# Down projection: fourteen of 22 pairs per half by seven products, their sums stored through GpSimd's queue, and weights laid out as tiles on the host

## The chip, the cores and the metric

The kernel runs on one core of one Trainium2 chip. The time is device time in microseconds (us). A core has TensorE (PE, matrix products into PSUM), VectorE (DVE), ScalarE (ACT), GpSimd (POOL) and SyncE (SP). DMAs are issued from the queues of SP, ACT and POOL and are carried out by 16 DMA engines. An engine executes its instructions in the order in which they were issued to it; a DMA queue issues its DMAs in order, and a DMA that waits holds up those behind it.

## The reference, cut to what matters

One layer of an encoder with batch 1, 256 tokens and 2048 features. Its last third is a gated channel mixer with a centred convolution of 3 taps over the tokens, a residual and a gate:

```python
def conv_glu(hn, w_up, conv_w, conv_b, w_down):      # hn (256, 2048), w_up (2048, 2*5632), w_down (5632, 2048)
    up = hn @ w_up
    gate, val = jnp.split(up, 2, axis=-1)
    gate = dwconv_centred(gate, conv_w, conv_b)      # 3 taps along the tokens, per feature
    return (jax.nn.gelu(gate, approximate=True) * val) @ w_down

# in the layer, after the mixer
hn = rmsnorm(h, ffn_norm_pre)
h = h + rmsnorm(conv_glu(hn, ...), ffn_norm_post)
gate = jax.nn.sigmoid(rmsnorm(h, ple_norm_pre) @ w_ple_gate)
h = h + rmsnorm(gate * (p @ w_ple), ple_norm_post)
```

`rmsnorm(x, g)` is x times 1/sqrt(mean of x squared over the features + 1e-6) times g. In front of this stands a mixer of a bidirectional state-space scan and a pooling part, with an input projection (`w_in`) and an output projection (`w_out`). All inputs are float32.

## The kernel before

**Products.** Each float32 operand is split into a high part, which TensorE's fp32r format holds, and the rest; a product of two operands is three products on PE (high x high, high x low, low x high). `split` (line 141) does this for a weight piece of up to 1024 columns: ACT copies the high part, DVE subtracts. The results lie in two pools of five buffers each, `whi` and `wlo`, that all weight pieces take in turn. The raw weights come through three buffers `raw` of 8 KB per partition.

**Stages.** In order: the input projection in three parts (`dtu`, `xbc`, `z`, 0 to 199 us of the span), the output projection `wo`, the embedding's first half `ple`, the up projection (293 to 789 us, eleven slabs of 512 gate features and 512 value features; `ga`, `va`), the down projection (`dn`, 789 to 1017 us, two halves of 1024 output columns), the embedding's second half, and the gate (`gt`, two halves).

**Up.** Each slab has two half slabs of gate and two of value features, computed features by tokens. `feature_pairs` (line 340) multiplies a half slab's weights, four splits, with the normalised input; after each two splits `aside` takes one list from `work` (line 194) and issues its jobs. `total` adds the two PSUM parts. The gate is multiplied by `rfb`, the row factor of the norm along the tokens; `conv` (line 416) applies the three taps, the middle one with the bias on ACT, the others as DVE scalar-tensor-tensor operations (line 428); ACT computes gelu; DVE multiplies the result by `rfb` (line 885), which belongs to the value half, and then by the value. The result stays in pages `hid` (features by tokens, six pages of 8 KB per partition).

**Down.** `token_major` (line 291) goes through 22 pairs of 128-row weight blocks for each half; its operand of 128 features by 128 tokens is the stationary one, 512 weight columns move. A regular pair takes 2 blocks x 2 token halves x 2 column halves x 3 = 24 products. For the pairs in `fast`, `seven_products` (line 239) treats the pair as a 2 x 2 block product and forms it with seven block products instead of eight (Strassen's scheme in Winograd's form), so 21 products; `combine` (line 269) then puts the accumulators right once for all of a half's such pairs. It needs four sums of activation blocks (`pair_sums`, line 774: four DVE operations on 128 columns, a split of 512 columns) and four sums of weight blocks (`add_blocks`, line 232).

The sums of weight blocks don't depend on the activations. For the down and gate pairs they are made during the up stage, as jobs in `work`: `block_sums` (line 208) has a `fetch`, two steps later an `add`, and one step later a `store` to DRAM, all DMAs on SP's queue; the last two stay in their pages. In the down stage a pair by seven products then loads its sums (a page of 1 MB, `t`) and the two blocks of raw weights that are used unsummed (1536 columns, two DMAs). The activation sums are made in `hid_sums` (line 920) when the pair comes, by DVE and ACT; those of the four pairs in `dn_keep` stay in two pages for the second half.

**Buffers.** There are 13 pages of 8 KB per partition for everything large, three buffers `mid` of 4 KB, two `hs` of 4 KB in the late part, and one `junk` of 2 KB.

**Order.** The source issues in program order, and a planner that works with expected times orders each engine's and each queue's instructions from it; `issue_after` and `load` (line 116) tie DMAs to the weight loads, except those marked as free to go ahead. `at` gives actions that are issued ahead of a pair: in the down stage's second half `back` at pair 13 (the residual `h` returns from DRAM, two DMAs of 1 MB) and `first_gate` at pair 16 (the first pair of gate weights: loaded once through SP, and once more by a POOL DMA that adds it to a negated copy, so that the low part is made without DVE; lines 943 to 952).

**DRAM layout.** The weights lie in DRAM as given. A tile of 128 partitions is gathered from rows of the matrix: pieces of 1 KB for the up weights, 2 KB for `xbc` and 4 KB for most others.

Of the kernel before, what the change touches and what calls it, by code (L numbers as in the profile page):

```python
# [11 lines left out]
F32 = mybir.dt.float32  # L12
# [39 lines left out]
def build(nc, a, out):  # L52
    x = a["x"][0]
    w_in, w_out, w_up = a["w_in"][0], a["w_out"][0], a["w_ffn_up"][0]
    w_down, w_gate, w_ple = a["w_ffn_down"][0], a["w_ple_gate"][0], a["w_ple"][0]
    out = out[0]

    with tile.TileContext(nc) as tc, \
# [37 lines left out]
        c_dt = DSSD + 1536  # L96
        r0 = wp.tile([P, 2048], F32, tag="raw", bufs=3, name="dtur0")
        for n in range(2):
            first = ins(nc.scalar.dma_start(r0[:, n * 352:(n + 1) * 352],
                                            w_in[:P, c_dt + n * 352:c_dt + (n + 1) * 352]))  # L100
# [55 lines left out]
        def raw(name, src, a_, b_):  # L156
            r = wp.tile([P, 2048], F32, tag="raw", bufs=3, name=name)
            if src is None:
                return r
            last["dma"] = load(r[:, :a_ * b_].rearrange("p (a b) -> p a b", a=a_), src, True)  # L160
            return r
# [46 lines left out]
        def block_sums(name, w, c0, k, held):  # L208


            pg = []

            def fetch():
                r = page(f"{name}b{c0}_{k}")
                pg.append(r)
                load(r.rearrange("p (k c) -> p k c", k=2),
                     w[k * P:(k + 2) * P, c0:c0 + 1024].rearrange("(k p) c -> p k c", p=P))

            def add():
                add_blocks(pg[0])  # L220
                if held:
                    sums_[name, c0, k] = pg[0], True

            def store():
                if not held:
                    t = dp.tile([P, 2048], F32, tag=f"{name}s{c0}_{k}", bufs=1, name=f"{name}s{c0}_{k}")
                    load(t, pg[0])
                    sums_[name, c0, k] = t, False

            return [fetch], [], [add], [store]  # L230

        def add_blocks(r):

            v = r.rearrange("p (b c) -> p b c", b=4)
            nc.vector.tensor_add(v[:, 0:2], v[:, 0:2], v[:, 1::2])  # L235
            nc.vector.tensor_add(v[:, 3], v[:, 3], v[:, 0])
            nc.vector.tensor_add(v[:, 2], v[:, 2], v[:, 3])

        def seven_products(name, stage, w, k0, c0, a_, acc, alt, start, stop):
# [3 lines left out]
            if (stage, c0, k0) in sums_:  # L243
                r = raw(f"{name}r", None, 0, 0)
                last["dma"] = load(r[:, 512:1536], w[(k0 + 1) * P:(k0 + 2) * P, c0:c0 + 1024], True)
                last["dma"] = load(r[:, :512], w[k0 * P:(k0 + 1) * P, c0:c0 + 512], True)
# [4 lines left out]
                b11 = split(f"{name}a", r[:, :512], 512)  # L251
                b2 = split(f"{name}b", r[:, 512:1536], 1024)
            else:
                r = t = raw(f"{name}r", w[k0 * P:(k0 + 2) * P, c0:c0 + 1024]
                            .rearrange("(k p) c -> p k c", p=P), 2, 1024)
                b11 = split(f"{name}a", r[:, :512], 512)
                b2 = split(f"{name}b", r[:, 1024:], 1024)
                add_blocks(r)
            t13 = split(f"{name}c", t[:, :1024], 1024)
            t42 = split(f"{name}d", t[:, 1024:], 1024)  # L260
            for x, (wh, wl), c, o, own in (
                    ("a11", b11, 0, alt[0], True), ("a12", b2, 0, acc[0][0], False), ("s4", b2, 512, acc[0][1], False),
                    ("s1", t13, 0, alt[1], True), ("s3", t13, 512, alt[2], True), ("a22", t42, 0, acc[1][0], False),
                    ("s2", t42, 512, alt[3], True)):
# [26 lines left out]
        def token_major(name, w, c0, ks, get, acc, tail=1, fast=(), alt=None, sums=None, at=()):  # L291
# [3 lines left out]
            for u in range(nu):  # L295
# [3 lines left out]
                if u in fast:  # L299
                    if u == fast[0]:  # L300
# [3 lines left out]
                r = None if f"{name}{k0}_0" in ready else raw(f"{name}r{k0}", w[k0 * P:(k0 + 2) * P, c0:c0 + 1024]  # L304
                                                               .rearrange("(k p) c -> p k c", p=P), 2, 1024)
# [8 lines left out]
                for t, (o, c), (k, wh, wl), q in order:  # L314
                    xh, xl = (v[:, t * P:(t + 1) * P] for v in get(k))
                    xx, ww = ((xh, wh), (xh, wl), (xl, wh))[q]
                    mm(o, xx, ww[:, c:c + o.shape[-1]], k == ks[0] and q == 0, k == ks[-1] and q == 2)
# [3 lines left out]
                aside()  # L321

        def feature_major(name, w, c0, get, acc):

            for u in range(4):
                r = raw(f"{name}r{u}", w[u * 512:(u + 1) * 512, c0:c0 + 512]
                        .rearrange("(k p) c -> p k c", p=P), 4, 512)
# [12 lines left out]
        def feature_pairs(name, w, c0, get, acc):  # L340


            for u in range(2):
                r = raw(f"{name}r{u}", w[u * 1024:(u + 1) * 1024, c0:c0 + 256]
                        .rearrange("(k p) c -> p k c", p=P), 8, 256)
# [97 lines left out]
        for u in range(0, NK, 2):  # L443
            r = [wp.tile([P, 2048], F32, tag="raw", bufs=3, name=f"dtur{u}") if u else r0, page(f"dtur{u + 1}")]
            for j in range(2):
                k = u + j
                if k == 0:
                    last["dma"] = load(r[0][:, 704:1056], w_in[:P, c_dt + 704:c_dt + 1056])
# [3 lines left out]
                for c0, c1 in ((0, 704), (704, 1056)) if k == 1 else ((0, 1056),):  # L452
                    last["dma"] = load(r[j][:, c0:c1], w_in[k * P:(k + 1) * P, c_dt + c0:c_dt + c1])
# [29 lines left out]
        with tc.issue_after(half[0]), tc.issue_after(half[1]):  # L483
# [11 lines left out]
            for a_ in range(4):  # L495
# [17 lines left out]
        load(pmat.rearrange("p (g s t) -> p g s t", g=4, s=2),  # L513
             a["pool_matrix"].rearrange("g (s p) t -> p g s t", p=P))
        poolw = page("poolw")
        load(poolw.rearrange("p (g c d) -> p g c d", g=4, c=2),
             a["pool_w"][0].rearrange("g (c p) d -> p g c d", p=P))
# [122 lines left out]
        def xbc(slab):  # L640
            acc = main(f"xbc{slab}")
            feature_major(f"xb{slab}", w_in, DSSD + slab * 512, hn, acc)
# [88 lines left out]
        token_major("z", w_in, 0, list(range(NK)), hn, zacc)  # L731
# [42 lines left out]
        def pair_sums(name, s, o, a11, a21, a12, a22):  # L774

            s1, s2, s3, s4 = (s[:, i * P:(i + 1) * P] for i in range(4))
# [5 lines left out]
            nc.vector.tensor_sub(o[:, 512:], s[:, :512], o[:, :512].bitcast(F32))  # L782
            return {f"s{i + 1}": (o[:, i * P:(i + 1) * P], o[:, 512 + i * P:512 + (i + 1) * P]) for i in range(4)}
# [22 lines left out]
        def sublayer(name, w, ks, get, gain, h, vnext, panel=Panel, fast=((), ()), sums=None, at=()):  # L806
# [3 lines left out]
            for half in range(2):  # L810
# [6 lines left out]
                for t in range(2):  # L817
                    for n in range(2):
# [4 lines left out]
                        nc.scalar.activation(junk, b, AF.Square, accum_out=q)  # L823
                        nc.vector.tensor_mul(mg[t][:, c], b, gain[:, c])
# [40 lines left out]
        dn_fast, gt_fast, dn_keep = ((2, 3, 5, 7, 8, 10, 12, 13, 15, 16, 18, 19), (2, 3, 5, 7, 8, 10, 12, 13, 15, 16, 18, 19)), ((4, 6), (1, 2)), (3, 8, 13, 18)  # L865
# [4 lines left out]
        for i, w_ in enumerate(which[2:] + which[:2]):  # L870
            for j, jobs in enumerate(block_sums(*w_, i >= len(which) - 2)):
                work[3 * i + 2 + j].extend(jobs)
        hid = []
        for s in range(DFF // 512):
            sc = mid(f"gr{s}")
            for i in range(2):
                ga = main(f"ga{s}{i}")
                feature_pairs(f"ug{s}{i}", w_up, s * 512 + i * 256, hf, ga)
# [4 lines left out]
            cv = conv(f"fc{s}", sc, 3, V_FCW + 4 * s, NF, V_FCB + 4 * s)  # L883
            nc.scalar.activation(cv, cv, AF.Gelu_apprx_tanh)
            nc.vector.tensor_tensor(cv.rearrange("p (f t) -> p f t", f=4), cv.rearrange("p (f t) -> p f t", f=4),
                                    rfb.unsqueeze(1).to_broadcast([P, 4, L]), op=ALU.mult)
            for i in range(2):
                va = main(f"va{s}{i}")
                feature_pairs(f"uv{s}{i}", w_up, DFF + s * 512 + i * 256, hf, va)
# [9 lines left out]
        def get_hid(k):  # L899
            if k % 2 == 0:  # L900
                t = lp.tile([P, 1024], F32R, tag="hs", bufs=2, name=f"hs{k}")
                src = hid[k // 8][:, (k % 8) * L:(k % 8 + 2) * L]
# [187 lines left out]
```

## Time and profile before

| | us |
|---|---|
| median of 3 runs | 1122.9 (1122.65 to 1123.32) |
| the profiled execution | 1123.46 |
| its span, first to last instruction | 1121.6 |

Busy time by stage in that execution, in us of the stretch:

| stretch | stage | PE | DVE | ACT | DMA share | GB/s |
|---|---|---|---|---|---|---|
| 0 to 50 | dtu | 48.5 | 26.7 | 37.6 | 0.99 | 369 |
| 50 to 143 | xbc | 92.2 | 76.1 | 61.4 | 0.45 | 152 |
| 143 to 199 | z | 56.0 | 46.9 | 28.5 | 0.59 | 207 |
| 199 to 293 | wo, ple | 94.0 | 83.3 | 52.5 | 0.60 | 190 |
| 293 to 789 | up | 495.5 | 400.7 | 257.4 | 0.93 | 307 |
| 789 to 903 | down, first half | 114.0 | 105.6 | 82.2 | 0.76 | 259 |
| 903 to 1017 | down, second half | 114.0 | 105.0 | 84.4 | 0.92 | 325 |
| 1017 to 1121 | ple, gate, end | 97.1 | 83.8 | 61.4 | | |

Matmul ends are modelled, so PE's busy share does not say that it runs at its full pace; the pace is read from the chain of waits, which gives the start of each string of products and their number. Line 87 is the helper that records every product, line 152 and 153 the two halves of `split`, line 119 every load; groups with these lines are told apart by the names of their tiles (`dn04ah`: half 0 of the down stage, block 4, first split, high part). The clock granted to PE was 0.999 on the mean.

### The profile page before, as it was taken

The numbers are of one execution on the slowest core, as the hardware profiler recorded it, in microseconds if no ns is written. First come the engines' busy times: TensorE is split into PE (matmuls) and PEld (weight loads), VectorE is DVE, ScalarE is ACT, GpSimd is POOL, SyncE is SP. The second block draws the span as 40 slices with busy tenths as digits, with TensorE's granted clock in tenths as the row PEclk, the third lists the DMA queues.
The fourth block names the chain that finished last, engine by engine and source line by source line (L and its number), as shares of the span: only waits on it lengthen the run. The fifth ranks groups of instructions, "written<-read, shape, count | busy, mean of one in ns | idle before, by whom it ended". The sixth has DMA issues, their size and how long they took to land.

```text
span 1121.6 us, 15747 instructions
## 1 busy us (share of the span) xinstructions
PE 1111.2 (99%) x5975; PEld 957.1 (85%) x5975; DVE 928.0 (83%) x1291; ACT 665.4 (59%) x929; POOL 31.1 (3%) x69
## 2 busy tenths in 40 slices
PE   9999999999999999999999999999999999999997
PEld 9999988888888888888888888888888888888876
DVE  6468897799898877877877768878799999899795
ACT  6848663555764554554545545545677777786673
POOL 0200000100100000000000000000000000001001
PEclk9999999999999999999999999999999999999999
DMA  9853447456799989999999898996969688995673
GB/s 361 312 197 104 162 161 277 151 188 189 252 320 349 316 298 340 303 295 313 341 319 310 289 335 303 313 297 218 321 198 336 219 292 295 381 323 175 231 235 107
DMA packets 145996, 300.87 MB, mean 268 GB/s; under 512 B 5504, under 2 KB 98560, under 8 KB 137856
## 3 DMA queue, kind: packets, MB, share of 16 engines
q1 hardware_dynamic: 145216, 298.19, 78.8%
q0 software_dynamic: 272, 1.05, 0.5%
q8 instruction: 47, 0.77, 0.3%
q10 hardware_dynamic: 432, 0.62, 0.2%
q14 instruction: 29, 0.24, 0.1%
HBM read 268.38 MB, written 31.46 MB: 267 GB/s over the span
## 4 chain that ended last, share of the span: by engine, by line
PE 95%; ACT 2%; DVE 1%; issue 1%; DMA 0%; POOL 0%; SPq 0%; POOLq 0%; ACTq 0%
PE va L87 22%; PE ga L87 21%; PE dna L87 14%; PE woa L87 7%; PE xbc L87 6%; PE gt L87 5%; PE z L87 4%; PE dtu L87 4%; PE dns L87 3%; PE dn0s L87 1%; PE dn1s L87 1%; PE ple L87 1%; PE pw L87 1%; PE yd L87 1%; DMA dtur<-w_in 0%
## 5 line engine op out<-in xcount | busy, mean ns | idle before, releaser
L87 PE MATMUL ga<-wox,ug_0h 128*128 128x512 f32 x352 | 125.5, 395 | 0.0
L87 PE MATMUL ga<-wox,ug_1h 128*128 128x512 f32 x352 | 125.1, 394 | 0.0
L87 PE MATMUL va<-wox,uv_1h 128*128 128x512 f32 x352 | 124.8, 393 | 0.0
L87 PE MATMUL va<-wox,uv_0h 128*128 128x512 f32 x352 | 124.8, 393 | 0.0
L87 PE MATMUL ga<-wox,ug_1l 128*128 128x256 f32 x352 | 99.2, 282 | 0.0
L87 PE MATMUL ga<-wox,ug_0l 128*128 128x256 f32 x352 | 99.1, 282 | 0.0
L87 PE MATMUL va<-wox,uv_1l 128*128 128x256 f32 x352 | 99.1, 281 | 0.0
L87 PE MATMUL va<-wox,uv_0l 128*128 128x256 f32 x352 | 99.1, 281 | 0.0
L87 PEld LDWEIGHTS va<-wox,uv_1h 128*128 128x128 f32 x352 | 66.1, 188 | 15.0
L87 PEld LDWEIGHTS va<-wox,uv_0h 128*128 128x128 f32 x352 | 66.1, 188 | 15.0
L87 PEld LDWEIGHTS ga<-wox,ug_0h 128*128 128x128 f32 x352 | 66.1, 188 | 14.9
L87 PEld LDWEIGHTS ga<-wox,ug_1h 128*128 128x128 f32 x352 | 66.1, 188 | 14.9
L87 PEld LDWEIGHTS ga<-wox,ug_0l 128*128 128x128 f32 x352 | 66.2, 188 | 0.1
L87 PEld LDWEIGHTS ga<-wox,ug_1l 128*128 128x128 f32 x352 | 66.2, 188 | 0.0
L87 PEld LDWEIGHTS va<-wox,uv_1l 128*128 128x128 f32 x352 | 66.2, 188 | 0.0
L87 PEld LDWEIGHTS va<-wox,uv_0l 128*128 128x128 f32 x352 | 66.2, 188 | 0.0
L87 PE MATMUL dna<-dn_0h,hs 128*128 128x512 f32 x160 | 50.1, 393 | 0.0
L87 PE MATMUL dna<-dn_1h,hs 128*128 128x512 f32 x160 | 49.9, 393 | 0.0
L235 DVE TENSOR_TENSOR dnb<-dnb 128x1024 f32<-128x1024 f32 x24 | 29.3, 1222 | 14.0 <-DMA dnb<-w_ffn_down 14.0
L903 ACT CAST hs<-hid 128x512 fp32r<-128x512 f32 x44 | 27.1, 617 | 18.3 <-PE dna L87 18.3
L904 DVE TENSOR_TENSOR hs<-hid,hs 128x512 fp32r<-128x512 f32 x44 | 30.2, 686 | 9.1 <-ACT hs L903 9.0
L428 DVE SCALAR_TENSOR_TENSOR fc<-gr,vt,fc 128x255 f32<-128x255 f32 x88 | 36.8, 479 | 0.1
(1909 smaller groups left out, 3060.3 us busy)
## 6 DMA issues: line engine op xcount, KB each, us to landing
dnb<-w_ffn_down SPq DMA_DIRECT2D x24, 1024.0 KB, 10.3
dns<-dnb SPq DMA_DIRECT2D x22, 1024.0 KB, 6.9
dn0r<-w_ffn_down SPq DMA_DIRECT2D x10, 1024.0 KB, 6.2
dn1r<-w_ffn_down SPq DMA_DIRECT2D x10, 1024.0 KB, 6.9
zr<-w_in SPq DMA_DIRECT2D x8, 1024.0 KB, 5.2
dtur<-w_in SPq DMA_DIRECT2D x14, 528.0 KB, 8.5
wo0r<-w_out SPq DMA_DIRECT2D x7, 1024.0 KB, 5.5
wo1r<-w_out SPq DMA_DIRECT2D x6, 1024.0 KB, 5.7
```

What stands on the lines that cost most here:

```text
L87: last["pe"] = ins(nc.tensor.matmul(o, lhsT, rhs, start=start, stop=stop, skip_group_check=True))
L235: nc.vector.tensor_add(v[:, 0:2], v[:, 0:2], v[:, 1::2])
L428: nc.vector.scalar_tensor_tensor(o[:, lo:hi], i[:, lo + d:hi + d], vec(wcol + j * wstep + f), o[:, lo:hi], op0=ALU.mult, op1=ALU.add)
L903: nc.scalar.copy(t[:, :512], src)
L904: nc.vector.tensor_sub(t[:, 512:], src, t[:, :512].bitcast(F32))
```

## The change

Six edits:

1. `dn_fast` has 14 pairs per half instead of 12, so runs of 4, 3, 3, 2 and 2 pairs. The products of a pair come in another order: the sums that were third and fourth in the split order change places, and the four products of `acc` are spread differently. `add_blocks` is four additions of 512 columns.
2. `block_sums` stores through POOL's queue. 30 of 32 sums are stored; the jobs lie 11/4 steps apart instead of 3. In the down stage a pair's raw weights are one DMA instead of two.
3. The activation sums of eight pairs (`dn_stored`) are made in the up stage, in an `hs` buffer, and stored by a POOL DMA of 0.5 MB; each half loads them again with a POOL DMA into a `mid` buffer. The other six pairs make theirs in each half, with `junk` as scratch. The two pages of `dn_keep` go.
4. The multiplication by `rfb` after gelu goes. The row factor comes in at the evacuation of the down projection, where a row is a token (`row=rf`).
5. The taps of the up stage are ACT operations with a scale into `cv`, `tp` and, in place, `sc`, and two DVE additions over two features, for each half slab as soon as it is done; gelu too goes by half slabs. `mid` has three users per slab instead of two.
6. All large weights are laid out on the host as tiles, so that a partition's 8 KB are contiguous (`pairs`: with the two 512-column parts of the first block exchanged, so that the 1536 columns that are used unsummed stand together). The first gate pair is loaded once, at pair 11, and split by ACT and DVE into pages; `back` comes after the last pair.

```diff
+        def raw(name, src=None):
             r = wp.tile([P, 2048], F32, tag="raw", bufs=3, name=name)
+            if src is not None:
+                last["dma"] = load(r, src, True)
             return r
...
             def fetch():
                 r = page(f"{name}b{c0}_{k}")
                 pg.append(r)
+                load(r, w[c0 // 1024, k // 2])
...
             def store():
-                if not held:
-                    t = dp.tile([P, 2048], F32, tag=f"{name}s{c0}_{k}", bufs=1, name=f"{name}s{c0}_{k}")
-                    load(t, pg[0])
-                    sums_[name, c0, k] = t, False
+                t = dp.tile([P, 2048], F32, tag=f"{name}s{c0}_{k}", bufs=1, name=f"{name}s{c0}_{k}")
+                nc.gpsimd.dma_start(t, pg[0])
+                sums_[name, c0, k] = t, False
...
-            nc.vector.tensor_add(v[:, 0:2], v[:, 0:2], v[:, 1::2])
-            nc.vector.tensor_add(v[:, 3], v[:, 3], v[:, 0])
-            nc.vector.tensor_add(v[:, 2], v[:, 2], v[:, 3])
+            for i, j in ((1, 0), (0, 3), (3, 1), (2, 3)):
+                nc.vector.tensor_add(v[:, i], v[:, i], v[:, j])
...
+                r = raw(f"{name}r")
+                last["dma"] = load(r[:, 512:], w[c0 // 1024, k0 // 2][:, 512:], True)
...
+            b11 = split(f"{name}a", r[:, 512:1024], 512)
+            b2 = split(f"{name}b", r[:, 1024:], 1024)
+            if r is t:
                 add_blocks(r)
-            t13 = split(f"{name}c", t[:, :1024], 1024)
             t42 = split(f"{name}d", t[:, 1024:], 1024)
+            t31 = split(f"{name}c", t[:, :1024], 1024)
             for x, (wh, wl), c, o, own in (
-                    ("a11", b11, 0, alt[0], True), ("a12", b2, 0, acc[0][0], False), ("s4", b2, 512, acc[0][1], False),
-                    ("s1", t13, 0, alt[1], True), ("s3", t13, 512, alt[2], True), ("a22", t42, 0, acc[1][0], False),
-                    ("s2", t42, 512, alt[3], True)):
+                    ("a11", b11, 0, alt[0], True), ("a12", b2, 0, acc[0][0], False), ("a22", t42, 0, acc[1][0], False),
+                    ("s4", b2, 512, acc[0][1], False), ("s2", t42, 512, alt[3], True), ("s1", t31, 512, alt[1], True),
+                    ("s3", t31, 0, alt[2], True)):
...
+                        if row:
+                            nc.scalar.activation(junk, b, AF.Square, scale=row[t], accum_out=q)
+                            nc.vector.scalar_tensor_tensor(mg[t][:, c], b, row[t], gain[:, c], op0=ALU.mult, op1=ALU.mult)
...
-        dn_fast, ... = ((2, 3, 5, 7, 8, 10, 12, 13, 15, 16, 18, 19), (the same)), ..., dn_keep = (3, 8, 13, 18)
+        dn_fast, ... = ((2, 3, 4, 5, 7, 8, 9, 11, 12, 13, 15, 16, 18, 19), (the same)), ...
+        dn_stored = (2, 3, 5, 8, 11, 13, 16, 19)
...
+            def make():
+                o.append(lp.tile([P, 1024], F32R, tag="hs", bufs=2, name=f"he{k}"))
+                hid_sums_of(k, o[0][:, 512:].bitcast(F32), o[0])
+            def store():
+                kept[k] = dp.tile([P, 1024], F32, tag=f"hsum{k}", bufs=1, name=f"hsum{k}")
+                nc.gpsimd.dma_start(kept[k], o[0].bitcast(F32))
...
-            cv = conv(f"fc{s}", sc, 3, V_FCW + 4 * s, NF, V_FCB + 4 * s)
-            nc.scalar.activation(cv, cv, AF.Gelu_apprx_tanh)
-            nc.vector.tensor_tensor(cv..., cv..., rfb.unsqueeze(1).to_broadcast([P, 4, L]), op=ALU.mult)
+                for f in range(2):
+                    w = V_FCW + 4 * s + 2 * i + f
+                    nc.scalar.activation(c[:, f], v[:, f], AF.Identity, bias=vec(V_FCB + 4 * s + 2 * i + f), scale=vec(w + NF))
+                    nc.scalar.activation(l[:, f], v[:, f], AF.Copy, scale=vec(w))
+                    nc.scalar.activation(v[:, f], v[:, f], AF.Copy, scale=vec(w + 2 * NF))
+                nc.vector.tensor_add(c[:, :, 1:], c[:, :, 1:], l[:, :, :L - 1])
+                nc.vector.tensor_add(c[:, :, :L - 1], c[:, :, :L - 1], v[:, :, 1:])
+                g = cv[:, i * 512:(i + 1) * 512]
+                nc.scalar.activation(g, g, AF.Gelu_apprx_tanh)
...
+            o = mid(f"hd{k}", F32R)
+            if k in kept:
+                nc.gpsimd.dma_start(o.bitcast(F32), kept[k])
...
+            r, hi, lo = page("gtf"), page("gtfh", F32R), page("gtfl", F32R)
+            last["dma"] = load(r, w_gate[0, 0])
             for j in range(2):
+                c = slice(j * 1024, (j + 1) * 1024)
+                spare[f"gt00_{j}"] = hi[:, c], lo[:, c]
+                ready[f"gt00_{j}"] = split(f"gt00_{j}", r[:, c], 1024)
...
-                      fast=dn_fast, sums=hid_sums, at={13: back, 16: first_gate})
+                      fast=dn_fast, sums=hid_sums, at={11: first, NF // 2: back}, row=rf)
...
+    def pairs(w):
+        r = tiles(w, 2, 1024)
+        return np.concatenate([r[..., 512:1024], r[..., :512], r[..., 1024:]], axis=-1)
```

## The prediction

> **What bounds the kernel now.** Read first the page's busy shares and then the table of stages: TensorE (PE) is busy in all of it, and in the two halves of the down projection (789 to 1017 us) VectorE (DVE) and the DMA engines are close behind.
>
> ```profile
> PE 1111.2 (99%) x5975; PEld 957.1 (85%) x5975; DVE 928.0 (83%) x1291; ACT 665.4 (59%) x929; POOL 31.1 (3%) x69
> ...
> 293.00:789.00 496.00, 495.45 (x2848) 434.70 (x2847) 400.71 (x527) 257.36 (x346) 1.48 (x4) 1.00 0.93 307
> 789.00:903.00 114.00, 114.00 (x496) 92.64 (x496) 105.59 (x147) 82.17 (x109) 0.00 (x0) 1.00 0.76 259
> 903.00:1017.00 114.00, 113.95 (x494) 92.29 (x493) 104.97 (x143) 84.39 (x109) 3.35 (x8) 1.00 0.92 325
> 953.00:973.00 20.00, 20.00 (x88) 16.23 (x87) 17.34 (x23) 14.65 (x19) 0.00 (x0) 1.00 1.01 411
> ```
>
> Columns: stretch, length, busy us and count of PE, weight loads, DVE, ACT, POOL, clock, DMA share, GB/s. Of 114 us, DVE works 105. The last row is the fullest 20 us of the second half: 411 GB/s, with PE not slowed.
>
> A modelled busy time does not prove a full pace, so next the chain of waits, which gives it.
>
> ```profile
> 789.10 11.11 PE dna L87 x48
> ...
> 891.64 22.16 PE dna L87 x96
> ...
> 1016.88 3.45 PE ple L87 x15
> ```
>
> 96 products in 22.16 us are 0.231 us each. Both halves together hold 20 regular pairs of 24 products and 24 pairs of 21, so 984: at 0.2312 us that is 227.5 us, and from 789.10 to 1016.88 are 227.8. No stall is left there to win. The up projection runs alike: every 128 products take 22.33 us.
>
> What each step costs comes from groups, timeline and DMA issues.
>
> ```profile
> 873.08 1.22 DVE L153 TENSOR_TENSOR dn_0l<-dn0r,dn_0h 128x1024 fp32r<-128x1024 f32 x1
> 874.22 1.22 DVE L153 TENSOR_TENSOR dn_1l<-dn0r,dn_1h 128x1024 fp32r<-128x1024 f32 x1
> 875.35 0.68 DVE L153 TENSOR_TENSOR dn036al<-dn036r,dn036ah 128x512 fp32r<-128x512 f32 x1
> 875.96 0.68 DVE L782 TENSOR_TENSOR he<-hd,he 128x512 fp32r<-128x512 f32 x1
> ...
> L780 DVE TENSOR_TENSOR hd<-hid,hd 128x128 f32<-128x128 f32 x17 | 4.9, 290 | 0.5
> ...
> L428 DVE SCALAR_TENSOR_TENSOR fc<-gr,vt,fc 128x255 f32<-128x255 f32 x88 | 36.8, 479 | 0.1
> ...
> L422 ACT ACTIVATE fc<-gr,vt 128x256 f32<-128x256 f32 x44 | 24.1, 594 | 12.0 <-DVE gr L882 11.9
> ...
> L949 POOL DMA_DIRECT2D gtfl<-w_ple_gate x1 | 1.4, 1426 | 670.2 <-ACT gtfl L948 670.2
> ...
> gtfl<-w_ple_gate POOLq DMA_DIRECT2D x1, 1024.0 KB, 14.4
> ...
> dn126r<-w_ffn_down SPq DMA_DIRECT2D x1, 512.0 KB, 11.0
> ```
>
> Durations overlap a little: back to back, DVE starts every 1.14 us at 1024 columns and every 0.61 at 512; I take 0.25 at 128. The last two lines are issue to landing, the first of them the only DMA that GpSimd (POOL) issues.
>
> **The change part by part**
>
> *Four more pairs by seven products.* Each drops 3 of 24 products: 12 x 0.2312 = 2.77 us of PE time, all on the path, as PE never waits there. Everything below asks whether PE stays fed.
>
> *DVE in the down stage.* A regular pair costs 2 x 1.14 + 0.61 = 2.9 us, a pair by seven products with stored activation sums 0.61 + 3 x 1.14 + 0.61 = 4.6, one that makes its sums 1.6 more (4 x 0.25 + 0.61), 6.25. The first half had 10 x 2.9 + 12 x 6.25 = 104 us (105.6 measured, with the evacuation); it gets 8 x 2.9 + 8 x 4.6 + 6 x 6.25 = 98. The second had 98, with 4 pairs kept, and gets 98 + 2.3 for the gate panel. PE's half is 8 x 5.55 + 14 x 4.86 = 112.4, so DVE stays below. In a run without regular pairs it does not: pairs 2 to 5 need 20.1 us in 19.4 of PE, 7 to 9 17.1 in 14.6, 11 to 13 15.5 in 14.6 (17.8 with the gate panel). The excess, 0.7 to 3.2 us, must be worked ahead; before, two making pairs in a row had 2 x 6.25 - 9.7 = 2.8 too much, and PE did not stall. Only the 3.2 lies beyond what the trace shows absorbed.
>
> *The new order of the seven products.* With five split buffers, the third split of a pair takes the buffer of the second of the pair before. That was free after product 9 (8 x 0.231 + 0.39 = 2.24 us) and wanted at product 10 of the next pair (4.86 + 2.08): 4.7 us for a 1.05 us ACT split and a 1.22 us DVE one. Now it is free after product 12 (2.94) and wanted at product 7 (6.25): 3.3 us, a margin of 1.0 instead of 2.4. A DVE that is one 1.14 us split late loses 0.14 us in each of the 18 pairs that follow another such pair, 2.5 us; on time it loses nothing. I take 0.2 in all, near the low end, because DVE's work per pair with stored sums (4.6) is still under PE's 4.86.
>
> *Activation sums, stored and read back.* Eight sums of 0.5 MB go out on POOL's queue in the up stage and come back in each half. The buffers are three, so pair 5's sums can be asked for when pair 2 ends, and are wanted at product 10 of pair 5: 2 x 4.86 + 2.08 = 11.8 us later; for all others a regular pair lies between, 17.4 us. The issue takes 1.43. The 0.5 MB loads of the down stage landed in 3.8 to 11.0 us, mostly about 6; the one POOL DMA in 14.4, but that was 1 MB that added into its target. So between 7.8 us early (taken with 3.8) and 1.43 + 14.4 - 11.8 = 4.0 late in each half, 0 to 8 us. I take 0: size and kind are those of the 6 us loads.
>
> *Bytes.* The second half moved 325 GB/s x 114 us = 37.1 MB. Two more pairs add 2 x 0.79 (1536 columns instead of 2048, and 1.05 of sums), the read sums 8 x 0.52 = 4.2, the second reading of the gate panel goes (1.05): 41.8 MB in 112.6 us, 371 GB/s. At the 411 of the fullest row it takes 102 us, at the half's own rate for a full share (325 / 0.92 = 353) 118. I take the first, since the low rate holds 1 to 4 KB pieces and the adding DMA, which vanish. [...]
>
> *GpSimd's queue.* 38 stores and 16 loads of 1.43 us each are 77 us on an engine that is busy for 31 of 1122. Behind them wait only the 1-column statistics. On SP the stores go, and with them 42.2 us (the waits of SP's queue) in which a store waited for DVE's line 237, with weight loads behind; PE lost nothing by that, so it gains nothing. Whether an issue on POOL holds DVE up, the trace can't tell: DVE was waiting for ACT during the only one. Between nothing and 8 x 1.43 = 11.4 us of DVE's time in a half, which it has idle (112.4 - 98 = 14), I take nothing; the far end makes the first rival likelier.
>
> *The up stage.* DVE loses 88 taps at 0.415 us (4 in 1.67) and 11 multiplications at 1.14 (49.0 us), and gains 44 additions at 0.61, 8 activation sums at 1.6 and, for 32 blocks at 4 x 0.61 instead of 28 at 2.36, another 12.0: 51.6. So 403 of 496 us. ACT gains 88 x 0.55 (2 in 1.09) and about 7 (gelu in halves 2, sums 5): 313 of 496. The cover is the four splits ahead, 4 x 2.79 = 11.2 us; the longest new burst is 6 x 0.55 = 3.3 us. Cost nothing; without cover it would be up to 3.3 us in each of 22 half slabs.
>
> *Moved loads.* The gate panel's 1 MB now stands on SP before pair 11's weights, 2.6 us at 411; ACT does 2.1 us for it instead of 3.8, DVE 2.3 instead of none. The two loads of the residual move behind the last down weights and stand before the weights of the per-layer embedding: 5.1 us for those. Before, these were issued at 999.3 and landed in 6.5; 5.1 later is 1010.9, and their splits (2.3) must end by 1014.1, which leaves 0.9 us. Nothing, with 2 us as the far end.
>
> *Host tiles, row factor.* Rows of 1 to 4 KB become 8 KB; where PE is full this is worth nothing. Only the start waits for a load (2.12 to 7.57 us); its pieces keep their length, so 0, at most 1.1 us (1.35 MB at 309 GB/s, the rate of 4 to 8 us, against 411). The evacuations with a row factor keep their 0.6 to 0.7 us.
>
> **Sum.** The profiled execution took 1123.46 us (span 1121.6), 0.5 over the median of 1122.9. 1123.46 - 2.77 + 0.2 = 1120.9; against the median 1120.3.
>
> **The rivals**
>
> *The feed is a little late.* The margins of 1.0 us, and the 3.2 us excess in pairs 11 to 13, cost 0.5 to 2.7 us: at 2.5 the time is 1122.6. For it: the halved margin. Against: DVE has 14 us of idle time per half.
>
> *POOL's sums land late.* At 14.4 us to landing, pair 5 waits 4.0 us in both halves: 1122.9 - 2.77 + 8.0 = 1128.1, slower. It decides from 11.8 - 1.43 = 10.4 us to landing, and loses the gain from 11.8. For it: the only row of that queue. Against: half the bytes, and no adding. [...]
>
> *The DMA engines bound the second half.* At 353 GB/s it lasts 118.4 us instead of 112.6: 1120.1 + 5.8 = 1125.9, slower. For it: 0.92 of a share already. Against: the 411 row, and whole rows.
>
> **How the numbers follow.** Forecast (PE-bound, 1119.0 to 1121.2) 0.58; feed late 0.23; sums late 0.10; DMA-bound 0.07; others 0.02, slower. A gain of 0.2%, about what a measurement of this kernel can tell, is 2.25 us, so the forecast may lose only 0.5: of its 0.58, 0.52 are faster and 0.06 the same. Feed late is the same in 0.22 and faster in 0.01. Faster 0.53, same 0.28, slower 0.19. The range runs from 1119.0 (start gained) to 1126.0 (DMA-bound) and leaves out the late sums and half of the rest.
>
> **What would show it.** Right: 972 products in 224.7 us, from the first down product to the embedding's first, in unbroken strings of 0.231; the up projection still 22.33 per 128; POOL's 0.5 MB landing under 10 us. Wrong: PE waiting for a DVE split of the third or fourth operand (feed); for the activation sums in pair 5 (late sums); ACT waiting for weight loads with DMA shares at 1.0 after 903 (bytes); a gap before the embedding's products (moved loads).

## The result: 1.0% slower, most of the loss in the up projection

The changed kernel takes 1134.6 us (median of 4 runs, 1132.35 to 1136.12) against 1123.0: 1.0102 times as long, 95% interval 1.0083 to 1.0121. The prediction was 1120.3, faster, with a range of 1119.0 to 1126.0. The profiled execution took 1136.12 (span 1134.4), 1.5 over the median.

The page of the changed kernel and the table of its stages (stretch, length, busy us and count of PE, weight loads, DVE, ACT, POOL, clock, DMA share, GB/s), to be laid beside those of before:

```profile
PE 1114.7 (98%) x5963; PEld 958.0 (84%) x5963; DVE 921.9 (81%) x1293; ACT 702.3 (62%) x1036; POOL 62.3 (5%) x122
...
293.00:804.00 511.00, 501.76 (x2847) 437.73 (x2847) 394.52 (x547) 289.71 (x451) 23.03 (x44) 0.99 0.85 325
804.00:916.00 112.00, 112.00 (x487) 91.07 (x486) 102.11 (x130) 84.45 (x107) 4.30 (x8) 1.00 0.83 316
916.00:1028.00 112.00, 112.00 (x487) 91.13 (x486) 105.84 (x137) 84.03 (x109) 8.11 (x12) 1.00 0.94 362
```

The down halves are 112 us, full of PE, as forecast. The up stage is longer (511 us instead of 496), PE is idle for 9 us of it, and the clock is below 1. By the starts of the first product of each stage, in the two profiled executions:

| stage | before | after | difference |
|---|---|---|---|
| start to first value product of up | 319.90 | 319.45 | -0.45 |
| from there to the first down product | 469.04 | 484.20 | +15.16 |
| down, both halves | 227.78 | 224.24 | -3.54 |
| end of down to the last 4 small products | 95.70 | 97.27 | +1.57 |
| rest | 9.18 | 9.20 | +0.02 |

The sum, 12.8 us, is the difference of the spans (1134.4 - 1121.6). The chain of waits of the changed kernel (start, us, what):

```profile
767.33 8.66 DMA hsum<-he
776.96 0.95 ACT uv_0h L151
777.94 1.24 DVE uv_0l L152
...
803.81 11.11 PE dna L88 x48
...
904.85 22.18 PE dna L88 x96
```

96 products in 22.18 us: the down stage runs at PE's pace. But the chain before it goes back to a store of activation sums. What PE waited for, in the whole span (total, times, longest; the three largest lines):

```profile
PE ga L88 <- DVE ug_1l L152: 3.2, 2, 1.9
PE va L88 <- ACT uv_0h L151: 2.7, 1, 2.7
PE va L88 <- DVE uv_1l L152: 2.3, 1, 2.3
```

These are weight splits of the up stage. There are four stalls (490, 679, 742 and 775 us); by the distances of the starts 9.9 us are lost in them. Of the other 5.3 of the 15.16 us, 3.7 are lost by the clock, also by the starts, and the rest in slips of a few tenths. The stall at 775, in stretches of 1 us (columns as above):

```profile
775.00:776.00 1.00, 0.25 (x2) 0.00 (x0) 0.00 (x0) 0.00 (x0) 0.00 (x0) 1.00 1.07 451
776.00:777.00 1.00, 0.00 (x0) 0.00 (x0) 0.28 (x1) 0.93 (x3) 0.00 (x0) 1.00 0.49 205
777.00:778.00 1.00, 0.04 (x1) 0.04 (x1) 0.81 (x3) 1.00 (x2) 0.00 (x0) 0.63 0.00 0
778.00:779.00 1.00, 0.75 (x1) 0.24 (x1) 1.00 (x1) 1.00 (x2) 0.00 (x0) 0.50 0.00 0
...
783.00:784.00 1.00, 1.00 (x5) 0.81 (x4) 0.98 (x3) 1.00 (x3) 0.00 (x0) 0.50 0.64 90
784.00:785.00 1.00, 1.00 (x7) 0.88 (x6) 1.00 (x2) 1.00 (x2) 0.00 (x0) 0.96 0.76 279
```

PE is empty for 2.7 us, and from 777.3 on it has half its clock for 6.8 us; after the stall at 490 it had half for 3.4 us. In front of the stall at 775 ACT had waited 7.9 us: a cast for the second down pair takes an `hs` buffer whose sums a store of 8.7 us was still reading. The last column says something more: from 777 to 779, while the splits catch up, the DMA engines move nothing. They do not hold the kernel up there; SP's queue waits for the same late splits (12.4 us for `uv_1l`).

Why the splits are late shows in the timeline around 490 us (start, us, engine, line, what; in brackets the idle time before it and what ended it):

```profile
479.24 0.33 SPq L118 DMA_DIRECT2D ug41r<-w_up  x1
479.63 0.42 SPq L118 DMA_DIRECT2D dnb<-w_down  x1
...
484.20 0.42 DVE L353 TENSOR_TENSOR hid<-hid,va 128x256 f32<-128x256 f32 x1
...
490.12 0.69 DVE L232 TENSOR_TENSOR dnb<-dnb 128x512 f32<-128x512 f32 x1 [5.50 <-DMA dnb<-w_down]
490.73 0.69 DVE L927 TENSOR_TENSOR hid<-hid,fc 128x512 f32<-128x512 f32 x1
491.33 1.22 DVE L152 TENSOR_TENSOR ug_1l<-ug41r,ug_1h 128x1024 fp32r<-128x1024 f32 x1
...
492.60 0.39 PE L88 MATMUL ga<-wox,ug_1l 128*128 128x256 f32 x1 [1.88 <-DVE ug_1l L152]
```

The down weights of a block (`dnb`) are asked for at 479.63 and land 10.4 us later. DVE has come to their additions after 5.0 us, and since it works in order it stands still for 5.5 us. The split `ug_1l` behind the addition needs none of that data, and PE waits for it. In the whole up stage DVE's waits for these blocks were, in the changed kernel,

```profile
DVE dnb L232 <- DMA dnb<-w_down: 59.9, 17, 7.2
DVE gtb L232 <- DMA gtb<-w_gate: 10.1, 2, 6.2
```

and before

```profile
DVE dnb L235 <- DMA dnb<-w_ffn_down: 14.0, 10, 4.0
DVE gtb L235 <- DMA gtb<-w_ple_gate: 5.0, 3, 3.9
```

Two measures, worked out from the timelines, sum this up. From the issue of a block's load to DVE's arrival at its additions there were 11.0 us before (median) and 7.5 after, while the loads of down blocks needed 10.3 and 9.1. And a split by DVE was ready 8.9 us (median; least 4.4, leaving out the stage's first 15 us) ahead of its first use by PE before, and 4.6 (least 0.06) after.

### The profile page after: what moved, and what is told of

Read it like the earlier page. It is cut to its first block, busy times and chain, and to the rows that moved or that the text cites. A ratio compares the mean times of both kernels' runs of the same rounds, so it can differ in the third digit from the quotient of the medians.

```text
span 1134.4 us, 15918 instructions
## 1 busy us (share of the span) xinstructions
PE 1114.7 (98%) x5963; PEld 958.0 (84%) x5963; DVE 921.9 (81%) x1293; ACT 702.3 (62%) x1036; POOL 62.3 (5%) x122
## 5 line engine op out<-in xcount | busy, mean ns | idle before, releaser
L88 PE MATMUL va<-wox,uv_0h 128*128 128x512 f32 x352 | 127.3, 399 | 2.7 <-ACT uv_0h L151 2.7
L232 DVE TENSOR_TENSOR dnb<-dnb 128x512 f32<-128x512 f32 x112 | 76.7, 687 | 60.7 <-DMA dnb<-w_down 59.9
L912 ACT ACTIVATE fc<-gr,vt 128x256 f32<-128x256 f32 x44 | 26.2, 595 | 71.0 <-DVE gr L907 71.0
L88 PE MATMUL dna<-dn_1h,hs 128*128 128x512 f32 x128 | 40.6, 393 | 0.0
L935 DVE TENSOR_TENSOR hs<-hid,hs 128x512 fp32r<-128x512 f32 x44 | 30.2, 686 | 12.8 <-ACT hs L934 12.8
L88 PE MATMUL dna<-dn_0h,hs 128*128 128x512 f32 x128 | 40.6, 393 | 0.0
```

Of the source, the lines that this page charges most:

```text
L88: last["pe"] = ins(nc.tensor.matmul(o, lhsT, rhs, start=start, stop=stop, skip_group_check=True))
L232: nc.vector.tensor_add(v[:, i], v[:, i], v[:, j])
L912: nc.scalar.activation(c[:, f], v[:, f], AF.Identity, bias=vec(V_FCB + 4 * s + 2 * i + f), scale=vec(w + NF))
L935: nc.vector.tensor_sub(t[:, 512:], hid_part(k), t[:, :512].bitcast(F32))
```

## The experiments

The loads were no slower than before, but DVE came to the additions sooner. The first theory took the distance in the job list (`fetch`, two steps later `add`) for the reason, with the wait of 7.9 us for the `hs` buffer as a second cause; the rivals were the DMA engines' rate, and the move of the stores to POOL's queue. Four runs test them.

**Additions a step later.**

```diff
-            return [[fetch], [], [add]] + [[store]] * (not held)
+            return [[fetch], [], [], [add]] + [[store]] * (not held)
```

> The changed kernel with one edit: each weight block's sums are added three steps of the up stage after their load is asked for, instead of two (about 5.6 us more). Theory A (the up stage loses its time because VectorE comes to the additions before their load has landed, waits in order, and the weight splits behind it come late): VectorE's idle time before these additions, 59.9 us for dnb in the changed kernel, falls below 15 us; the stalls of TensorE at 490, 679 and 742 us, 6.0 us of empty time and 1.7 us of half clock, go; the stall at 775 us (7.3 us with its half clock) stays. Up stage about 477 us instead of 484.2, time about 1127. Rival B (the DMA engines are the limit of the up stage): the wait only moves, to ScalarE's wait for up weights; the time stays within 1132 to 1136.

Measured: 1133.4 us (ratio 1.0097, 1.0082 to 1.0111); DVE still waited 50.2 us for `dnb`, from issue to arrival there were still 7.5 us. A miss, and in the end an empty experiment: in DVE's order of instructions the additions hardly moved. The job list fixes when a job is handed in; where it then stands in the engine's order is the planner's choice. That order can be put into a number. A block's load stands on SP behind the m-th weight load of the up stage, and that load needs the raw buffer which weights m - 3 occupied, so 2(m - 3) splits must be done. If the additions stand behind the n-th split, n - 2(m - 3) splits lie between the issue of the load and the additions; PE consumes one in 2.79 us (22.33 / 8). The mean over the blocks (without the first three) was 4.4 before, 3.3 after the change, and 3.4 here.

**Pair 19's sums not stored,** alone and with the edit above.

```diff
-        dn_stored = (2, 3, 5, 8, 11, 13, 16, 19)
+        dn_stored = (2, 3, 5, 8, 11, 13, 16)
```

> The changed kernel with pair 19 left out of the stored activation sums: seven stores instead of eight, and pair 19 makes its sums in each half like pair 18. Theory A, second part (ScalarE stood 7.9 us at 768 us because a cast for the second down pair takes the hs buffer whose sums, of pair 19, were still being stored by a DMA of 8.7 us; TensorE lost 3.9 us empty and 3.4 us by half clock): that stall goes, the three at the additions stay or move; time about 1127 to 1129. In the down stage two pairs in a row that make sums cost nothing, as before. Rival B (DMA limit): 0.5 MB less in 162 MB, so no change: 1132 to 1136.

> Both edits together: additions three steps after the load, and pair 19's activation sums not stored. Theory A: both causes go; up stage 469 to 471 us as before the change, down stage 224.3, time 1120 to 1122 (the predicted 1120.3 and up to 1.6 more for the gate stage), faster than before the change by 0.1 to 0.3%. Rival B (DMA limit): 1130 or more.

Measured: 1132.2 us (1.0080, 1.0067 to 1.0093) and 1130.0 (1.0065, 1.0051 to 1.0079). Both miss theory A, which said 1127 to 1129 and 1120 to 1122. In their times both agree with rival B, the DMA limit; the tied kernel further below speaks against it: its DMA engines move 336 GB/s between 320 and 788 us, against 324 in the changed kernel. The wait for an `hs` buffer did not go; the planner put the second down pair's cast right behind the sums that were now the last, and ACT stood there for 8.6 us at 702. DVE's waits for the blocks stayed (54.8 us for `dnb` in the first of the two, 61.3 in the second).

**Stores on SP again.**

```diff
-                nc.gpsimd.dma_start(t, pg[0])
+                load(t, pg[0])
```

> The changed kernel with the weight sums stored through SP's queue again, as before the change; nothing else changed. Theory C (the move of the stores is what made the loads late: on SP a load stood right behind the store of the block before it and was asked for when that block's additions ended, 11 us ahead of its own additions; without the store it stands behind a weight load and is asked for only 5 to 8 us ahead): VectorE's wait for dnb falls to about 15 us, the three stalls go, time about 1127. If the closer spacing of the blocks (11/4 steps instead of 3) or the taps on ScalarE are the cause, the waits stay above 40 us and the time stays at 1132 to 1136.

Measured: 1121.0 us, 0.9982 of the time before (0.9973 to 0.9991). This one line is worth 13.6 us, more than theory C had expected of it. The up stage takes 469.2 us, as before the change, and DVE's wait for `dnb` is

```profile
DVE dnb L232 <- DMA dnb<-w_down: 0.7, 1, 0.7
```

Now 6.0 splits lie between load and additions, and 13.2 us from issue to arrival. ACT's wait of 7.9 us for the `hs` buffer doesn't occur here either. Nothing else of the change was undone: the closer blocks, the taps on ACT and the stored activation sums cost the up stage nothing. The lead of DVE's splits is still only 5.6 us here (median; least 0.09), and PE does not wait for one: a short lead is a risk, and the loss comes only when a wait eats the rest of it.

That leaves two ways in which POOL's queue could do it: by its transfers, which run beside SP's loads, or only by the order in which the planner then puts the instructions. The landing times (median) of the stores differ:

```profile
dns<-dnb POOLq DMA_DIRECT2D x26, 1024.0 KB, 8.6
```

is a line of the page of the changed kernel; with the stores on SP the answer for the tile `dns` in the up stage is

```profile
L118 SPq DMA_DIRECT2D dns<-dnb x26: 326/326/327, 321.3 to 677.4; - x26
...
DMA to landing us min/median/max: 3.8/4.9/9.9
```

So in these two kernels a store of 1 MB lands 3.7 us later on POOL's queue, and the loads of `dnb` hardly later: in 8.5 us with the stores on SP, 9.1 with them on POOL.

**Stores on POOL, additions tied.** The next kernel keeps POOL's stores and fixes only the order: the additions must stand behind the last weight split that stood ahead of their load in the program.

```diff
                 load(r, w[c0 // 1024, k // 2])
+                pg.append(last["dve"])
...
             def add():
-                add_blocks(pg[0])
+                with tc.issue_after(pg[1]):
+                    add_blocks(pg[0])
```

> The changed kernel with its stores still on POOL's queue, but each block's additions tied behind the last weight split that stands ahead of its load, so that VectorE's order has them as late as with the stores on SP (6 weight splits behind the load's issue for most blocks, instead of 3). Theory P (the planner, with the stores off SP's queue, expects the loads earlier than they land and puts the additions too early in VectorE's order; the transfers themselves are no slower): VectorE's wait for dnb falls from 59.9 us below 15, the up stage is 469 to 472 us, the time 1121 to 1124, as with the stores on SP. Rival Q (the transfers of POOL's queue take the loads' turns at the DMA engines): the up stage stays at 478 us or more, the time at 1130 or more, with ScalarE waiting for up weights.

Measured: 1121.05 us (0.9982, 0.9973 to 0.9991), the same as with the stores on SP. The up stage takes 469.04 us, to a hundredth as before the change; DVE does not wait for a block at all, its splits are again 8.9 us ahead (median; least 1.4). The stores still land in 8.5 us and the blocks in 8.9. The transfers on POOL's queue cost the up stage nothing; the order did it all. ACT's wait for the `hs` buffer is still there (7.0 us at 753) and costs nothing: with the splits ahead by their full lead, it is hidden. It was the second blow to a lead that DVE's waits had used up.

**The same two steps on the kernel before.**

```diff
-                    load(t, pg[0])
+                    nc.gpsimd.dma_start(t, pg[0])
```

> The kernel before the change with one edit: the weight sums are stored through POOL's queue. In VectorE's order the additions then stand 3.1 weight splits behind the issue of their load instead of 4.4. Theory P: this alone makes VectorE wait for dnb 40 us or more instead of 14, the least lead of VectorE's splits over TensorE falls from 4.4 us to under 1, and the time rises to 1126 to 1135. Rival R (POOL's stores harm only together with the closer blocks or the taps on ScalarE): 1122.5 to 1123.5.

and then with the additions tied in the same way:

> The kernel before the change with its stores on POOL's queue (1136.9 us) and the additions tied as in the tied kernel (5.4 weight splits behind the issue of their load on the mean, instead of 3.1). Theory P: the whole loss goes, 1122.5 to 1123.5, and VectorE waits for dnb less than 15 us. Rival Q (POOL's transfers, here with rows of 4 KB, take turns from the loads): 1127 or more.

Measured: 1136.9 us with the stores on POOL (1.0126, 1.0112 to 1.0140), 2 us beyond the range expected, and 1123.07 with the additions tied as well (0.9999, 0.9990 to 1.0008). The up stage takes 485.8 us in the first and 469.04 in the second. The first kernel's waits of DVE in the up stage:

```profile
DVE dnb L235 <- DMA dnb<-w_ffn_down: 87.9, 20, 7.8
DVE gtb L235 <- DMA gtb<-w_ple_gate: 15.5, 3, 7.1
```

and all that is left of them with the tie:

```profile
DVE gtb L237 <- DMA gtb<-w_ple_gate: 0.7, 1, 0.7
```

The move of one store line, on a kernel that has nothing else of the change, costs 13.9 us, and a tie that changes no work takes all of it back. With 3.1 splits between load and additions, the kernel before loses about as much as the changed one with 3.3. The stores' landing differs little here: 6.9 us (median) on SP's queue before, and 7.7 and 6.9 on POOL's in these two runs.

**What the other parts are worth.** Stores on SP, with 12 pairs per half at three steps (and pair 11, which is no longer fast, out of the stored sums):

```diff
-        dn_fast = ((2, 3, 4, 5, 7, 8, 9, 11, 12, 13, 15, 16, 18, 19), (the same))
+        dn_fast = ((2, 3, 5, 7, 8, 10, 12, 13, 15, 16, 18, 19), (the same))
-        dn_stored = (2, 3, 5, 8, 11, 13, 16, 19)
+        dn_stored = (2, 3, 5, 8, 13, 16, 19)
...
-                work[11 * i // 4 + 0 + j].extend(jobs)
+                work[3 * i + 2 + j].extend(jobs)
```

> Stores on SP and the 12 pairs per half of the kernel before (28 blocks, three steps apart, stored activation sums for seven of the eight pairs). The term of 12 x 0.2312 = 2.77 us: the down stage takes 227.0 us instead of 224.24, so the time is 1123.8. If the feed binds the down stage after all, the difference is smaller.

Measured: 1122.2 us (0.9992, 0.9983 to 1.0001), 1.6 less than expected. The down stage takes 226.95 us instead of 224.24: the 12 products are worth 2.71, as worked out. But the time differs by 1.14 only, because the gate stage takes 95.68 us with 12 pairs and 97.32 with 14. So the second loss hangs on something that this run undid, the 14 pairs, the closer blocks or pair 11's stored sums, although nothing of the gate stage itself was changed.

**The residual asked for earlier,** in the 14-pair kernel with the stores on SP:

```diff
-                      fast=dn_fast, sums=hid_sums, at={11: first, NF // 2: back}, row=rf)
+                      fast=dn_fast, sums=hid_sums, at={11: first, 20: back}, row=rf)
```

> Stores on SP (the kernel of 1121.0 us) and the residual's reload asked for ahead of pair 20 of the second half instead of behind the last pair. Theory G (the gate stage takes 1.6 us more than before, 97.3 instead of 95.7, because the embedding's load stands behind the two loads of the residual, and its splits and the gate's are placed behind the evacuation): the gate stage takes 95.7 to 96 us again and the time is 1119.3 to 1119.8. If the evacuation with the row factor is the cause, it stays at 97.3 and 1121.0. If the earlier reload takes pages from the stored sums, the down stage gets longer than 224.3.

Measured: 1121.8 us (0.9989, 0.9980 to 0.9998). The gate stage gains 0.5 us (96.83), the down stage loses 1.3 (225.51): the two loads now stand ahead of the last down weights. No gain. The embedding's first split stands 10.6 us ahead of the end of the down stage here, as early as before the change, and still the gate stage is 1.1 us longer than before: an early split alone does not bring it back.

**The residual on POOL's queue,** in the tied kernel:

```diff
-                last["dma"] = load(h[t], h_kept[t])
+                nc.gpsimd.dma_start(h[t], h_kept[t])
```

> The kernel with stores on POOL and tied additions (1121.05 us), and the two loads of the residual (back) moved from SP's queue to POOL's. In the 14-pair kernels the embedding's load landed 9.2 us ahead of the end of the down stage, but ScalarE's order had its first split 1.8 us ahead of that end, against 10.8 us before the change. Theory P in the gate stage (the planner expects SP's loads later than they land, behind the residual's 2 MB, and places the embedding's and the gate's splits too late): with the residual off SP the splits come up to 10 us earlier, the gate stage takes 95.7 us instead of 97.3, the time is 1119.4, 0.3% faster than before. Rival E (the loads are late on the chip, behind the residual's 2 MB): the gate stage also gets shorter, but only if the embedding's load lands earlier than 9.2 us ahead of the end. If neither, 1121.0.

Measured: 1119.7 us, 0.9970 of the time before (0.9958 to 0.9982), the fastest of all. The gate stage takes 95.83 us. ACT's timeline at the end of the down stage (which is at 1012.50), in the tied kernel:

```profile
1008.56 0.69 ACT L821 ACTIVATE dnj<-dna,rf0r 128x512 f32<-128x512 f32 x1 [6.86 <-PE dna L88]
...
1010.67 1.04 ACT L151 CAST ple_0h<-ple1r 128x1024 fp32r<-128x1024 f32 x1
```

and with the residual on POOL's queue (end of the down stage at 1012.39):

```profile
1003.01 1.05 ACT L151 CAST ple_0h<-ple1r 128x1024 fp32r<-128x1024 f32 x1 [1.10 <-DMA ple1r<-w_ple_]
...
1008.45 0.69 ACT L821 ACTIVATE dnj<-dna,rf0r 128x512 f32<-128x512 f32 x1
```

In the first kernel ACT stands idle for 6.86 us, in the last 5.3 of them with the embedding's weights in its reach (they landed 9.2 us ahead of the end of the stage), because the first square of the evacuation stands ahead of their split. In the second they landed 9.5 us ahead, so hardly sooner, but their split stands first. Again it is the order, and not the transfer: the residual itself landed no sooner (its second load at 1001.05 us, against 1000.82 in the tied kernel). With the late splits PE waited 1.1 us for `gt_0l`, most of the 1.5 us; that wait is gone here.

## Why the prediction was wrong, step by step

**Four more pairs by seven products: right.** 12 products were priced at 2.77 us, and the comparison of the two 14- and 12-pair kernels gives 2.71. The down stage gained 3.54 in all. One product of the embedding that lay in it before (0.23) has moved out. The remaining 0.6 us was not forecast, so it is luck; the 12-pair kernel has it too (226.95 us, against 227.55 without that product), so it does not come from the two pairs more. 0.3 of it is a slip of PE in the trace before, at 987 us; of the rest no run shows the cause.

**DVE and the split buffers in the down stage: right,** and a little too careful. PE never waited for a split there in the changed kernel; the 0.2 us taken for the margins were not lost, nor the 2.5 of the first rival.

**Activation sums read back: right.** The 16 loads on POOL's queue landed in 4.0 to 10.0 us, below the 10.4 from which they would have decided; but the median was 8.0, where the prediction had counted on about 6, so the margin was smaller than thought.

**Bytes: right.** The second half moved 362 GB/s at a share of 0.94 and PE did not wait. The third rival's 353 was no limit: 362 was held over 112 us, and 451 for 1 us at 775. That rows of 8 KB made the difference was the author's estimate; no run has them alone.

**GpSimd's queue: this is the step that failed.** It said "On SP the stores go ... PE lost nothing by that, so it gains nothing" and looked at what stands behind a store on its new queue, what SP's queue gains, and what an issue costs (1.43 us priced; 0.53 measured for the stores). All of that was harmless. The term was put at nothing and cost 13.6 us. What it did not ask is what the planner makes of the move: the description of the kernel names it as the one that sets every engine's order, and yet the order was taken as given. With the stores off SP, the additions stood 3.3 instead of 4.4 splits behind their loads, DVE waited 70 us instead of 19 for blocks, and the lead of its splits was gone. The order can be counted ahead of a run: for the kernel before with POOL's stores, untied and tied, the expectations gave 3.1 and 5.4 splits, and the traces have them.

**The up stage: right in its terms, wrong in its conclusion.** In the fastest kernel, where the stage has its old length, DVE was busy for 401 us (403 estimated) and ACT for 293 (313 estimated). "Cost nothing" rested on a cover of 11.2 us against bursts of 3.3 us of work. The cover was 8.9 us in the median and 4.4 at the least, and what used it up was no burst of work but a place too early in DVE's order, and the waiting there. Among the signs of being right stood "the up projection still 22.33 per 128"; that sign failed, and only the 0.02 of "others, slower" stood for it.

**Moved loads: wrong, with the far end not far off.** Nothing was taken, 2 us kept as the far end; the gate stage lost 1.57 (0.23 of it the moved product). The loads landed in time, as the margin of 0.9 us promised (9.4 us ahead of the end of the down stage). The split stood only 1.8 us ahead of it, behind the first squares of the evacuation, and PE then waited 1.1 us for `gt_0l`.

**Host tiles and the row factor: right.** Up to the first value product the changed kernel needed 319.45 us against 319.90, but the variants of both kernels lie between 319.1 and 320.5, so no gain is shown. The evacuation cost nothing: the 12-pair kernel has the row factor and a gate stage of 95.68 us.

**The rivals.** None of the three was it. The slower one that came nearest, POOL's sums late, looked at the right queue but at the loads of the down stage. A rival with a chance of its own was missing: that the order in the up stage changes and DVE waits.

That the planner expects the loads to land earlier when the stores are off SP, and later when the residual stands on it, is argued: the runs show the order it chose, not its estimate. Both moves also drop the tie to the last weight load that `load` sets, which a plain DMA on POOL doesn't have; whether the planner answered to the queue or to the lost tie, no run separates. Shown is that the order alone makes the difference, since the tie, which moves no work, takes the loss back in two kernels. For the gate stage one pair of runs shows the gain with the split ahead of the evacuation and the load landing when it did, but the residual asked for earlier had the split ahead as well and gained only 0.5 us there; its cause is not shown in full.

## What to carry to other kernels

Where a scheduler orders the engines, an edit of a queue is an edit of every engine's order: compare the orders of both kernels for each wait on a DMA, and count what lies between the issue of the load and the first instruction that needs it. An in-order engine that reaches optional work early makes urgent work late (here DVE stood 5.5 us at an addition, and PE 1.9 us for the split behind it); tie the optional work behind urgent work rather than moving its job; the transfers can stay where they are. And when a change of many parts comes out wrong, undo the parts one at a time: here one line of six edits held 13.6 us.

## What the runs showed of the hardware

Two short stalls of PE cost more by the clock. In the changed kernel an empty time of 1.9 us at 490 was followed by 3.413 us at a granted clock of 0.50, one of 2.7 us at 775 by 6.827 us, twice as long; one of 2.3 us at 742 by none.

The trace shows a pattern. The half clock starts at 493.95, 777.25 and 1128.83 us in the changed kernel: 283.30 and 351.58 us apart, 83 and 103 times the 3.413 us of the first one. Lay steps of that length over the traces of the changed kernel and of the one before from 20 us on (in the second by its only start, 1118.38), and take the empty time from PE's busy time in the trace: each of the four steps at full clock in which PE was empty for 1.87 us or more was followed by half clock, and none of those with 1.53 or less was. The 1.9 us at 490 lie within one step; the 2.3 us at 742 are cut into 1.2 and 1.1. The half clock that began at 777.25 lasted a second step, and PE was empty for another 1.2 us in its first; the one from 493.95, without empty time, lasted one. So in these two traces the limit lies between 1.53 and 1.87 us of empty time in a step, and where a stall of 2 us falls decides whether more is lost: by an estimate up to 1.7 us, half of the 3.413 at half clock.

Stores of 1 MB landed in medians of 4.9 to 6.9 us on SP's queue and 6.9 to 9.2 on POOL's, depending on the kernel around them; the loads beside them took 8.1 to 10.3 and 8.6 to 10.4 us. An issue on POOL took 0.53 us for the stores, where the one DMA of the trace before, which adds into its target, had taken 1.43.
